# Two model blocks on one core: the high halves of a unit's weights multiplied first, retention keys in blocks of 128, 128 and 16, the last job's halves in one go, and three ring tiles for early expert chunks

## The chip, the core and the metric

The kernel runs on one core of a Trainium2 chip. The core has a matrix engine (PE, with PEld for its weight loads), a vector engine (DVE), a scalar engine (ACT), a general engine (POOL) and a queue engine (SP) that issues most of the transfers; 16 DMA engines move the data. The metric is the device time of one launch in microseconds (us). The profile is one further execution of the same program.

## The reference, cut to what matters

Everything is in float32. The first block takes 256 tokens behind 16 meta tokens (T = 272 rows of 1024) and the second block takes the 256 tokens that come out.

```
def first_block(...):                          # one layer
    u = rmsnorm(h, mix_norm_w);  proj = u @ w_in
    q, k, v, g_ret, lru_in, lru_gate, gate_a, gate_b = split(proj)
    q, k = rotary(q), rotary(k) * 128 ** -0.5          # 8 heads of 128
    o = chunk_retention(q, k, v)                        # causal, decay per head
    y_ret = (silu(g_ret) * head_norm(o)) @ w_branch_ret
    y_lru = (gelu(lru_gate) * rg_lru(conv(lru_in))) @ w_branch_lru
    h = h + (sigmoid(gate_a) * y_ret + sigmoid(gate_b) * y_lru) @ w_out
    g, up = split(rmsnorm(h, ffn_norm_w) @ w_ffn_in)
    h = h + (silu(g) * up) @ w_ffn_out
    return rmsnorm(h, final_norm_w)[:, 16:]

def second_block(x, ...):                      # one layer
    h = x + hybrid_mixer(rms_norm(x), ...)     # mLSTM and a gated spatial mix, then w_out
    # 32 experts (1024 -> 512 -> 1024) in 4 groups, 2 experts per token
    h = h + hierarchical_moe(rms_norm(h), ..., w_gate, w_up, w_down)
    return rms_norm(h, final_g)
```

Without its chunks, one head of retention is: row t of the output is the sum over s <= t of decay^(t-s) (q_t . k_s) v_s, for 272 keys and the 256 queries that are kept.

## The kernel before, in words

**The dense part** holds all of the first block and the second block's mixer, to about 632 us. Its weights are stored as chunks of 1 MB that SP loads in order into a ring of five tiles, `raw` (`load_to`, L147). A chunk is two units of 128 x 1024. ACT rounds a unit to `whi` (L161, four buffers), and DVE, or POOL for units 2 and 5, subtracts that from the chunk to get `wlo` (L167, three buffers). A unit is 24 matmuls on PE: for each of eight slices k of the contraction, the high half of the weights times the high half of the input, the high half times the input's low half, and the low half times the input's high half (`mm3`, L233). `proj` calls `mm3` for some 124 of the units; the others use code of their own. What a unit's result needs afterwards runs behind a later unit.

In the first units the input itself is split slice by slice, by ACT (`FR`, L278) and DVE (L279), while PE uses it. POOL also multiplies the rotary tables COS and SIN by a norm (L290, L291) before it splits unit 5.

**Retention** runs with two heads interleaved, in four pairs, between units. `f0` multiplies K and Q, `f1` scales and masks the products on ACT and DVE into `sw`, and `f2` multiplies by the values. The 272 keys stand as 16 + 128 + 128, the 16 keys of the meta tokens first, so each head has five matmuls in `f2`: 16, 128, 16, 128 and 128 keys deep.

**The expert part** streams the chosen experts' weights, 1 MB chunks again, in one fixed order on SP (`ex`, L1078). A chunk takes the next of 18 fresh buffers, which are tiles that the dense part has finished with (four `raw2`, `FR2`, `FR3`, then `xg`, `yy` and `lb` of a pool that opens late, five ring `raw` tiles, `FR1`, and three pairs of `whi` and `wlo` tiles); after the 18th it takes a buffer that a finished job has given back. `before_wo(i)` calls `ex` between the last dense units. A job is one chunk column (g, c) for a group of tokens: c from 0 to 3 are the gate and up products (L1683), 4 and 5 the down products (L1710 to L1717) followed by scaling (L1736, L1737) and a matmul that adds the rows back into the residual (L1746 to L1748). The first job is (0, 0).

**The end.** The last job is done in two halves of 256 columns. Then the final norm takes sums of squares (L1650 on DVE, L1652 on ACT), POOL multiplies the residual by the gain (L1656), the sums are added (L1779, L1780), root and reciprocal follow, the rows are scaled (L1921 to L1926) and four transfers go out on SP (L1928).

Of the kernel before, what the change touches and what calls it, by code (L numbers as in the profile page):

```python
# [11 lines left out]
F32 = mybir.dt.float32  # L12
# [9 lines left out]
D = 1024  # L22
# [17 lines left out]
HOLD = 5  # L40
WARM = 16
# [58 lines left out]
def _build(tc, nc, h, out, ctx, dbg, stop):  # L100
# [156 lines left out]
    RST = PA.tile([128, TT], F32, name="RST")  # L257
    SP.dma_start(COS, h["rope"][0])
# [35 lines left out]
    def proj(xh, xl, c0, n, *stages, adv=1, tag=None, before=None, ps=ps_mm):  # L294

        o = {}

        def mm(hi, lo):
            p = o["p"] = ps()
            for k in range(8):  # L300
                mm3(p[:, :n], hi[:, k * 128:k * 128 + 128], lo[:, k * 128:k * 128 + 128],
                    xh[:, k, c0:c0 + n], xl[:, k, c0:c0 + n], k == 0, k == 7)
        unit(mm, [lambda f=f: f(o["p"]) for f in stages], adv, tag=tag, before=before)
# [116 lines left out]
    def v_evac(m):  # L420
# [6 lines left out]
        def g(p):  # L427
            t = o["t"]
            q = o["q"] = ps_tp()
            PE.transpose(q[:, 0:128], t[:, NM:NM + 128], ident)  # L430
            PE.transpose(q[:, 128:256], t[:, NM + 128:], ident)
            PE.transpose(q[0:NM, 256:384], t[:, 0:NM], ident)
# [81 lines left out]
    def ret(hd):  # L514
        o = {}
        e = slice(hd * 128, hd * 128 + 128)

        def f0():
            p = o["p"] = ps_sa()
            p2 = o["p2"] = ps_tp()  # L520
            PE.matmul(p[:, 0:256], K[:, hd, NM:NM + 128], Q[:, hd], start=True, stop=True)
            PE.matmul(p[:, 256:384], K[:, hd, NM + 128:], Q[:, hd, 128:], start=True, stop=True)
            PE.matmul(p2[0:NM, 0:256], K[:, hd, 0:NM], Q[:, hd], start=True, stop=True)

        def f1():
            p, p2 = o["p"], o["p2"]
            w = o["w"] = PA.tile([128, 384], F32, name="sw", bufs=2)
            wm = o["wm"] = PA.tile([NM, 256], F32, name="swm", bufs=2)
            S.activation(w[:, 128:256], p[:, 128:256], AF.Copy, scale=vt("gk", 8 + hd))
            S.activation(wm, p2[0:NM, 0:256], AF.Copy, scale=vt("gk", hd)[0:NM])  # L530
            V.scalar_tensor_tensor(w[:, 0:128], p[:, 0:128], vt("gk", 8 + hd), tri, OP.mult, OP.mult)
            V.scalar_tensor_tensor(w[:, 256:384], p[:, 256:384], vt("gk", 16 + hd), tri, OP.mult, OP.mult)

        def f2():
            w, wm = o["w"], o["wm"]
            p = o["p"] = ps_sa()
            PE.matmul(p[:, 0:128], wm[:, 0:128], VM[:, e], start=True, stop=False)
            PE.matmul(p[:, 0:128], w[:, 0:128], VV[:, 0, e], start=False, stop=True)
            PE.matmul(p[:, 128:256], wm[:, 128:256], VM[:, e], start=True, stop=False)
            PE.matmul(p[:, 128:256], w[:, 128:256], VV[:, 0, e], start=False, stop=False)  # L540
            PE.matmul(p[:, 128:256], w[:, 256:384], VV[:, 1, e], start=False, stop=True)
# [470 lines left out]
    for g in range(NG):  # L1012
# [22 lines left out]
                  + [lambda n=n: [fl2(P0.tile([128, 8, TT], F32, name=n))] for n in ("FR2", "FR3")]  # L1035
                  + [lambda: [fl(B["PD"].tile([128, 8, 256], F32, name="xg", bufs=2))],
                     lambda: [fl(B["PD"].tile([128, 4, 512], F32, name="yy"))],
                     lambda: [B["PD"].tile([128, 2048], F32, name="lb")]]
                  + [lambda: [ring.tile([128, 2048], F32, name="raw")]] * RING
# [4 lines left out]
    once = (RING2 + 2, RING2 + 3)  # L1044
# [293 lines left out]
    def before_wo(i):  # L1338
        def f():
            ex(RING2 + 2)  # L1340
            if i == 4:
                need("x1")
                lg["p"] = ps_tp()
        return f
# [299 lines left out]
    def squares(i, c0, n):  # L1644

        for t in range(2):
            x = HB[:, t, c0:c0 + n]
            jk = fl(PD.tile([128, 2, T], F32, name="sg", bufs=2))[:, 0:n]
            if t:
# [101 lines left out]
    def group_job(g, c):  # L1751
# [164 lines left out]
    for t in range(2):  # L1916
        S.activation(rq[:, t:t + 1], rf[:, t, 2:3], AF.Sqrt, scale=1.0 / D, bias=rf[:, t, 0:1])
    for t in range(2):
        r = rq[:, t:t + 1]
        V.reciprocal(r, r)  # L1920
        S.activation(HB[:, t, 0:512], HB[:, t, 0:512], AF.Copy, scale=r)  # L1921
        V.scalar_tensor_tensor(HB[:, t, 768:1024], HB[:, t, 768:1024], r, fing[:, 768:1024], OP.mult, OP.mult)  # L1922
        if t:
            S.activation(HB[:, t, 512:768], HB[:, t, 512:768], AF.Copy, scale=r)
        else:
            V.tensor_scalar(HB[:, t, 512:768], HB[:, t, 512:768], r, None, OP.mult)  # L1926
        for c in (slice(0, 512), slice(512, 1024)):
            SP.dma_start(out[0, t * 128:t * 128 + 128, c], HB[:, t, c])  # L1928
# [35 lines left out]
def pack(inp):  # L1964
    f = np.float32
    a = {k: np.asarray(v) for k, v in inp.items()}
    for k in a:
        if k not in ("x", "meta_tokens", "final_norm_w", "final_g_2"):
# [37 lines left out]
    gk = np.stack([np.exp(-(p - mid)[:, None] * lg), np.exp(-(p + NM - mid)[:, None] * lg),  # L2006
                   np.exp(-(p + NM + 128 - mid)[:, None] * lg)], axis=1) * 128.0 ** -0.5
# [71 lines left out]
```

## Time and profile before

| what | before |
|---|---|
| three runs, median | 1061.01 us (1057.22, 1061.01, 1061.42) |
| profiled execution, its own time | 1060.79 us |
| its span in the trace | 1059.1 us |
| PE busy in the span | 968.0 us (91%) |
| DVE, ACT, POOL busy | 530.3, 408.4 and 64.2 us |
| moved by DMA | 294.96 MB, mean 279 GB/s |

The span is the stretch that the trace covers; the execution's own time is 1.7 us longer. Busy time is the sum over the whole span, which holds two stretches of different kind: the dense part to about 632 us and the expert part after it.

### The profile page before, as it was taken

Reading aid. Unit: us, or ns where it says so; the run is one execution under the profiler, and the core shown is the slowest. Engines: PE = TensorE matmul, PEld = TensorE weight load, DVE = VectorE, ACT = ScalarE, POOL = GpSimd, SP = SyncE. Lnnn points to the kernel's source line nnn. Section 1 sums busy time; section 2 is a strip of 40 time slices with the busy share of each in tenths; the row PEclk is TensorE's granted clock in tenths of the full one; section 3 lists DMA queues with packets and bytes.
Section 4 is the critical chain, followed back from the end, with each engine's and each line's share of the span. In section 5 each row is a group of like instructions: output and inputs, shape, how many; then the busy total and the mean of one; then the engine's idle time right before and its main releaser. Section 6 shows DMA issues by size and latency. Waiting matters only on the chain. (4 is left out here: it accounts for less than half of the span.)

```text
span 1059.1 us, 19506 instructions
## 1 busy us (share of the span) xinstructions
PE 968.0 (91%) x7888; PEld 766.0 (72%) x7888; DVE 530.3 (50%) x961; ACT 408.4 (39%) x682; POOL 64.2 (6%) x63
## 2 busy tenths in 40 slices
PE   8999999999999999999999999989689768878674
PEld 7999998899999999999988985535344324424222
DVE  6788684467777666666796834322112202112013
ACT  6466863466455444444576632111001000100003
POOL 2137400010000000000200000000000000000001
PEclk9999999999999999999999999999898998989978
DMA  8454453336556555545465599999999999999995
GB/s 340 163 192 164 166 193 120 120 110 234 180 195 218 200 178 181 199 167 192 160 227 211 201 375 419 416 416 416 415 418 416 418 418 416 419 416 418 418 417 200
DMA packets 48378, 294.96 MB, mean 279 GB/s; under 512 B 5397, under 2 KB 7061, under 8 KB 17562
## 3 DMA queue, kind: packets, MB, share of 16 engines
q1 hardware_dynamic: 47992, 293.25, 71.1%
q8 instruction: 64, 1.05, 0.4%
q10 hardware_dynamic: 290, 0.39, 0.1%
q14 instruction: 32, 0.26, 0.1%
HBM read 305.16 MB, written 1.05 MB: 289 GB/s over the span
## 5 line engine op out<-in xcount | busy, mean ns | idle before, releaser
L233 PE MATMUL mm<-FR,whi 128*128 128x256 f32 (+1 forms) x2080 | 380.8, 285 | 3.3 <-ACT FR L278 1.8
L233 PEld LDWEIGHTS mm<-FR,whi 128*128 128x128 f32 x2080 | 323.6, 190 | 6.5 <-ACT FR L278 2.0
L167 DVE TENSOR_TENSOR wlo<-raw,whi 128x1024 fp32r<-128x1024 f32 x188 | 237.8, 1268 | 141.0 <-PE mm L233 73.5
L233 PE MATMUL mm<-FR,wlo 128*128 128x256 f32 (+1 forms) x1040 | 295.4, 284 | 1.5 <-POOL wlo L167 0.8
L161 ACT ACTIVATE whi<-raw 128x1024 fp32r<-128x1024 f32 x190 | 200.2, 1059 | 199.8 <-PE mm L233 144.3
L233 PEld LDWEIGHTS mm<-FR,wlo 128*128 128x128 f32 x1040 | 197.9, 190 | 2.0 <-POOL wlo L167 1.0
L1683 PE MATMUL sa<-raw,xg 128*32 128x256 f32 (+1 forms) x1168 | 150.0, 422 | 23.1 <-DMA raw<-in_we_dram 23.1
L1683 PEld LDWEIGHTS sa<-raw,xg 128*32 128x32 f32 (+1 forms) x1168 | 72.5, 126 | 66.4 <-DMA raw<-in_we_dram 31.2
L1683 PE MATMUL sa<-FR,xg 128*32 128x256 f32 (+1 forms) x448 | 74.6, 424 | 16.2 <-DMA FR<-in_we_dram 16.2
L1694 ACT ACTIVATE ht<-tp 128x128 f32<-128x128 f32 x40 | 11.1, 278 | 178.4 <-PE tp L1693 178.4
L1748 DVE TENSOR_TENSOR XS<-mm,XS 128x512 f32<-128x512 f32 (+1 forms) x42 | 26.0, 660 | 86.4 <-PE mm L1747 86.4
L1737 DVE SCALAR_TENSOR_TENSOR yy<-mm,ws,yy 128x512 fp32r<-128x512 f32 (+1 forms) x20 | 14.7, 735 | 104.3 <-ACT yy L1736 104.3
L1683 PE MATMUL sa<-whi,xg 128*32 128x256 f32 (+1 forms) x272 | 62.2, 410 | 2.2 <-DMA whi<-in_we_dram 2.2
L1683 PEld LDWEIGHTS sa<-FR,xg 128*32 128x32 f32 (+1 forms) x448 | 34.6, 125 | 36.0 <-DMA FR<-in_we_dram 21.8
L1689 DVE TENSOR_TENSOR sg<-sg,sa 128x128 f32<-128x128 f32 x40 | 11.3, 283 | 78.2 <-ACT sg L1688 78.2
L233 PE MATMUL mm<-FL,whi 128*128 128x256 f32 x176 | 49.9, 284 | 0.0
L233 PE MATMUL mm<-FH,wlo 128*128 128x256 f32 x176 | 49.8, 283 | 0.0
L233 PE MATMUL mm<-FH,whi 128*128 128x256 f32 x176 | 49.8, 283 | 0.0
L341 PE MATMUL mm<-FR,whi 128*128 128x256 f32 x256 | 46.5, 283 | 0.0
L1688 ACT ACTIVATE sg<-sa 128x128 f32<-128x128 f32 x40 | 11.0, 276 | 85.7 <-PE sa L1683 85.4
L233 PE MATMUL mm<-whi,FR 128*128 128x512 f32 x128 | 41.5, 406 | 0.0
L341 PEld LDWEIGHTS mm<-FR,whi 128*128 128x128 f32 x256 | 39.2, 188 | 0.6 <-issue 0.5
(460 smaller groups left out, 1449.4 us busy)
## 6 DMA issues: line engine op xcount, KB each, us to landing
raw<-in_we_dram SPq DMA_DIRECT2D x106, 1024.0 KB, 15.0
raw<-in_wd_dram SPq DMA_DIRECT2D x94, 1024.0 KB, 4.9
FR<-in_we_dram SPq DMA_DIRECT2D x35, 1024.0 KB, 17.4
whi<-in_we_dram SPq DMA_DIRECT2D x46, 512.0 KB, 16.2
lb<-in_we_dram SPq DMA_DIRECT2D x12, 1024.0 KB, 14.9
wlo<-in_we_dram SPq DMA_DIRECT2D x22, 512.0 KB, 14.9
raw<-in_we_dram SPq DMA_DIRECT2D x4, 512.0 KB
raw<-in_wd_dram SPq DMA_DIRECT2D x2, 512.0 KB
```

The source lines that it names most:

```text
L161: S.activation(his[u], half(u), AF.Copy)
L167: (G if u in POOL_LO or u - 2 * nch in POOL_LO else V).tensor_tensor(los[u], half(u), his[u].bitcast(F32), op=OP.subtract)
L233: PE.matmul(o, a, b, start=start and i == 0, stop=stop and i == 2)
L341: PE.matmul(p[:, j * T:j * T + T], w[:, b:b + 128], z[:, k, 0:T], start=k == 0 and j == 0 and x == 0, stop=k == 7 and x == 2, skip_group_c ...
L1683: PE.matmul(p[r, 0:256], x[:, k, r], raw(k * 256, k * 256 + 256), start=k == 0, stop=k == 7)
L1688: S.activation(sg[:, 0:128], p[:, 0:128], AF.Silu)
L1689: V.tensor_tensor(sg[:, 128:256], sg[:, 0:128], p[:, 128:256], op=OP.mult)
L1694: S.activation(ht()[:, c], q[:, 0:128], AF.Copy)
L1737: V.scalar_tensor_tensor(yl, p[:, 0:n], ws[:, 0:1], yh.bitcast(F32), OP.mult, OP.subtract)
L1748: V.tensor_tensor(HB[:, t, c0:c0 + n], o[:, 0:n], HB[:, t, c0:c0 + n], op=OP.add)
```

## The change: what it does

Six edits are made together.

- **A.** `load_to(3)` is called before the loads of COS, SIN and CS.
- **B.** In `proj`, a unit's 16 matmuls with the high half of its weights stand first, and its 8 with the low half after them; nothing else about the products changes.
- **C.** Retention's keys are taken as 128 + 128 + 16. `f0` has moving sizes of 256, 144 and 16 columns in place of 256, 128 and 256. `f1` scales and masks five blocks in place of four and clears two small ones on POOL. `f2` keeps five matmuls of 128 columns a head: 128 keys, 128 keys for the last 32 rows, 128, 128, and 16 keys for the last 32 rows. The table of decays `gk` and the values' transposes are ordered to suit.
- **D.** `EARLY = 3`: three of the five ring `raw` tiles stand ahead of `xg`, `yy` and `lb` among the fresh buffers, and `before_wo(2)` to `before_wo(4)` may each issue one of them.
- **E.** In the last job the second half's matmuls stand ahead of the first half's adding back; the load of the root's table stands earlier; POOL takes the gain for the first 512 columns alone; the two small additions of sums are gone.
- **F.** The final norm has one sum over the three partial sums, one root and one reciprocal for both row blocks; ACT scales 512 columns and DVE scales the other 512 with the gain; one of the four output transfers is issued by ACT.

```diff
+EARLY = 3
...
+    load_to(3)
     SP.dma_start(COS, h["rope"][0])
...
         def mm(hi, lo):
             p = o["p"] = ps()
+            b = lambda w, k: w[:, k * 128:k * 128 + 128]
             for k in range(8):
-                mm3(p[:, :n], hi[:, k * 128:k * 128 + 128], lo[:, k * 128:k * 128 + 128],
-                    xh[:, k, c0:c0 + n], xl[:, k, c0:c0 + n], k == 0, k == 7)
+                for i, x in enumerate((xh, xl)):
+                    PE.matmul(p[:, :n], b(hi, k), x[:, k, c0:c0 + n], start=k == 0 and i == 0, stop=False)
+            for k in range(8):
+                PE.matmul(p[:, :n], b(lo, k), xh[:, k, c0:c0 + n], start=False, stop=k == 7)
...
         def f0():
             p = o["p"] = ps_sa()
-            p2 = o["p2"] = ps_tp()
-            PE.matmul(p[:, 0:256], K[:, hd, NM:NM + 128], Q[:, hd], start=True, stop=True)
-            PE.matmul(p[:, 256:384], K[:, hd, NM + 128:], Q[:, hd, 128:], start=True, stop=True)
-            PE.matmul(p2[0:NM, 0:256], K[:, hd, 0:NM], Q[:, hd], start=True, stop=True)
+            PE.matmul(p[:, 0:256], K[:, hd, 0:128], Q[:, hd], start=True, stop=True)
+            PE.matmul(p[:, 256:400], K[:, hd, 128:256], Q[:, hd, 112:], start=True, stop=True)
+            PE.matmul(p[0:NM, 400:416], K[:, hd, T:], Q[:, hd, T - NM:], start=True, stop=True)
...
+            G.memset(w[:, 256:272], 0.0)
+            G.memset(w[0:NM, 416:432], 0.0)
+            S.activation(w[:, 112:256], p[:, 112:256], AF.Copy, scale=gA)
+            S.activation(w[:, 400:416], p[:, 384:400], AF.Copy, scale=gB)
+            V.scalar_tensor_tensor(w[:, 0:112], p[:, 0:112], gA, tri[:, 16:128], OP.mult, OP.mult)
+            V.scalar_tensor_tensor(w[:, 272:400], p[:, 256:384], gB, tri, OP.mult, OP.mult)
+            V.scalar_tensor_tensor(w[0:NM, 432:448], p[0:NM, 400:416], gC, tri[0:NM, 0:NM], OP.mult, OP.mult)
...
         def f2():
...
-            PE.matmul(p[:, 0:128], wm[:, 0:128], VM[:, e], start=True, stop=False)
-            PE.matmul(p[:, 0:128], w[:, 0:128], VV[:, 0, e], start=False, stop=True)
-            PE.matmul(p[:, 128:256], wm[:, 128:256], VM[:, e], start=True, stop=False)
-            PE.matmul(p[:, 128:256], w[:, 128:256], VV[:, 0, e], start=False, stop=False)
-            PE.matmul(p[:, 128:256], w[:, 256:384], VV[:, 1, e], start=False, stop=True)
+            last = slice(96, 128)
+            PE.matmul(p[:, 0:128], w[:, 0:128], VV[:, 0, e], start=True, stop=False, skip_group_check=True)
+            PE.matmul(p[last, 0:128], w[:, 256:288], VV[:, 1, e], start=False, stop=True, skip_group_check=True)
+            PE.matmul(p[:, 128:256], w[:, 128:256], VV[:, 0, e], start=True, stop=False, skip_group_check=True)
+            PE.matmul(p[:, 128:256], w[:, 288:416], VV[:, 1, e], start=False, stop=False, skip_group_check=True)
+            PE.matmul(p[last, 128:256], w[0:NM, 416:448], VM[:, e], start=False, stop=True, skip_group_check=True)
...
+                  + [lambda: [ring.tile([128, 2048], F32, name="raw")]] * EARLY
                   + [lambda: [fl(B["PD"].tile([128, 8, 256], F32, name="xg", bufs=2))],
...
-                  + [lambda: [ring.tile([128, 2048], F32, name="raw")]] * RING
+                  + [lambda: [ring.tile([128, 2048], F32, name="raw")]] * (RING - EARLY)
...
-            ex(RING2 + 2)
+            ex(RING2 + 2 + max(0, min(i - 1, EARLY)))
...
         mm, e0, e1 = down_steps(hts[g], *prep[g], 512, 256)
+        V.memset(rq, 1.0)
+        S.activation(rq, rq, AF.Sqrt)
         mm(parts)
         flush()
         e0()
-        V.memset(rq, 1.0)
-        S.activation(rq, rq, AF.Sqrt)
         mm_, e0_, e1_ = down_steps(hts[g], *prep[g], 768, 256, exact=True)
-        e1()
         mm_(parts)
         squares(0, 0, 512)
         gain(0, 512)
-        squares(1, 512, 256)
-        gain(512, 256)
-        x = rf[:, :, 0]
-        V.tensor_tensor(x, x, rf[:, :, 1], op=OP.add)
-        V.tensor_scalar(x, x, 1.0 / D, EPS, OP.mult, OP.add)
-        return e0_, e1_
+        e0_()
+        e1()
+        squares(1, 512, 256, True)
+        return (e1_,)
...
-    for t in range(2):
-        S.activation(rq[:, t:t + 1], rf[:, t, 2:3], AF.Sqrt, scale=1.0 / D, bias=rf[:, t, 0:1])
+    V.tensor_reduce(rq, rf, AX.X, OP.add)
+    S.activation(rq, rq, AF.Sqrt, scale=1.0 / D, bias=vt("eps"))
+    V.reciprocal(rq, rq)
     for t in range(2):
         r = rq[:, t:t + 1]
...
+        a, b = slice(0, 512), slice(512, 1024)
+        S.activation(HB[:, t, a], HB[:, t, a], AF.Copy, scale=r)
+        V.scalar_tensor_tensor(HB[:, t, b], HB[:, t, b], r, fing[:, b], OP.mult, OP.mult)
+        for i, c in enumerate((a, b)):
+            (S if t and not i else SP).dma_start(out[0, t * 128:t * 128 + 128, c], HB[:, t, c])
```

Where two heads' `f2` stand on PE, these are one head's five matmuls before (the last column is the weights' partitions by the moving columns).

```order
L537 MATMUL sa<-VM,swm 128x128
L538 MATMUL sa<-VV,sw 128x128
L539 MATMUL sa<-VM,swm 128x128
L540 MATMUL sa<-VV,sw 128x128
L541 MATMUL sa<-VV,sw 128x128
```

The same place on PE after the change.

```order
L546 MATMUL sa<-VV,sw 128x128
L547 MATMUL sa<-VV,sw 32x128
L548 MATMUL sa<-VV,sw 128x128
L549 MATMUL sa<-VV,sw 128x128
L550 MATMUL sa<-VM,sw 32x128
```

The number of matmuls and their moving columns stay, two of them now write 32 rows, and the one 16 keys deep stands last alone instead of at two places.

On SP, where the last dense chunks give way to the first expert chunks, the loads stood like this (`in_wd` are dense chunks, `in_we` expert chunks).

```order
L147 DMA raw<-in_wd_dram 128x2048 x2
L1078 DMA raw_6603<-in_we_dram 128x2048
L1078 DMA FR_6605<-in_we_dram 128x2048
L1078 DMA FR_6607<-in_we_dram 128x2048
L1078 DMA xg<-in_we_dram 128x2048
L1078 DMA yy<-in_we_dram 128x2048
L1078 DMA lb<-in_we_dram 128x2048
L1078 DMA raw<-in_we_dram 128x2048 x5
L1078 DMA FR_6892<-in_we_dram 128x2048
```

After the change they stand like this.

```order
L1088 DMA raw_6611<-in_we_dram 128x2048
L1088 DMA FR_6613<-in_we_dram 128x2048
L1088 DMA FR_6615<-in_we_dram 128x2048
L1088 DMA raw<-in_we_dram 128x2048 x3
L1088 DMA xg<-in_we_dram 128x2048
L1088 DMA yy<-in_we_dram 128x2048
L1088 DMA lb<-in_we_dram 128x2048
L1088 DMA raw<-in_we_dram 128x2048 x2
L1088 DMA FR_6900<-in_we_dram 128x2048
```

Three loads into ring tiles now stand ahead of those into `xg`, `yy` and `lb`; the number of loads before the first reuse of a buffer is the same.

## Rows read from the trace of the kernel before

**Rows 1.** The page: 40 slices of the span, busy tenths.

```profile
PE   8999999999999999999999999989689768878674
DMA  8454453336556555545465599999999999999995
```

**Rows 2.** Windows: engine busy us (x), granted PE clock, DMA share, GB/s.

```profile
595.00:600.50 5.50, 5.50 (x50) 5.50 (x49) 5.27 (x8) 4.69 (x7) 0.58 (x1) 1.00 0.02 6
...
633.00:634.00 1.00, 1.00 (x24) 0.63 (x20) 0.92 (x5) 0.70 (x2) 0.00 (x0) 1.00 0.53 78
...
634.00:1041.00 407.00, 335.39 (x2928) 161.98 (x2919) 84.72 (x236) 43.92 (x128) 0.00 (x0) 0.93 1.01 416
```

**Rows 3.** Timeline of SP's queue, 586 to 634 us: start, us, issue.

```profile
618.57 2.67 SPq L1078 DMA_DIRECT2D wlo<-in_we_dram  x2
632.63 0.80 SPq L1078 DMA_DIRECT2D raw<-in_we_dram  x2
```

**Rows 4.** Timeline of PE, 628 to 634 us.

```profile
628.96 3.66 PE L1683 MATMUL sa<-raw,xg 128*32 128x256 f32 x64
```

**Rows 5.** PE's waits, 0 to 632 us: us in total, times, longest.

```profile
PE tp L233 <- POOL wlo L167: 1.1, 1, 1.1
...
PE mm L233 <- DVE wlo L167: 1.0, 2, 0.7
```

**Rows 6.** Timeline of DVE (first row) and PE, 7 to 18 us.

```profile
8.43 3.40 DVE L279 SCALAR_TENSOR_TENSOR FR<-XS,VT,FR 128x272 fp32r<-128x272 f32 x8
...
12.29 0.52 PE L233 MATMUL mm<-FR,whi 128*128 128x272 f32 x2
13.55 0.40 PE L233 MATMUL mm<-FR,wlo 128*128 128x272 f32 x1 [0.74 <-DVE wlo L167]
...
16.05 0.42 PE L233 MATMUL mm<-FR,whi 128*128 128x272 f32 x2
...
16.43 0.41 PE L233 MATMUL mm<-FR,whi 128*128 128x272 f32 x2
17.64 0.39 PE L233 MATMUL mm<-FR,wlo 128*128 128x272 f32 x1 [0.79 <-POOL wlo L167]
```

**Rows 7.** Timeline of PE: a pair's `f0` at 186, part of its `f2` at 195.

```profile
186.41 0.59 PE L521 MATMUL sa<-Q,K 128*128 128x256 f32 x2
186.84 0.38 PE L522 MATMUL sa<-Q,K 128*128 128x128 f32 x2
187.16 0.60 PE L523 MATMUL tp<-Q,K 128*16 128x256 f32 x2
187.69 0.70 PE L521 MATMUL sa<-Q,K 128*128 128x256 f32 x2
...
195.78 0.48 PE L539 MATMUL sa<-VM,swm 16*128 16x128 f32 x2
196.20 0.49 PE L540 MATMUL sa<-VV,sw 128*128 128x128 f32 x2
196.52 0.39 PE L541 MATMUL sa<-VV,sw 128*128 128x128 f32 x2
196.84 0.48 PE L537 MATMUL sa<-VM,swm 16*128 16x128 f32 x2
```

**Rows 8.** Window around the second pair's `f2`.

```profile
178.00:184.00 6.00, 6.00 (x36) 5.76 (x36) 1.08 (x3) 1.16 (x7) 0.00 (x0) 0.72 0.43 164
```

**Rows 9.** Timeline of the end, 1047 to 1055 us.

```profile
1047.70 3.57 POOL L1656 TENSOR_TENSOR XS<-XS,H 128x1024 f32<-128x1024 f32 x2 [446.17 <-DVE sg L1650]
...
1048.10 1.97 DVE L1779 TENSOR_TENSOR rf<-rf 128x2 f32<-128x2 f32 x1 [0.29 <-ACT sg L1652]
...
1048.87 1.13 PE L1744 MATMUL mm<-sg,pm 128*128 128x256 f32 x4 [0.56 <-ACT sg L1733]
...
1051.21 0.74 DVE L1748 TENSOR_TENSOR XS<-mm,XS 128x256 f32<-128x256 f32 x2
...
1054.26 0.49 ACT L1924 ACTIVATE XS<-XS,rq 128x256 f32<-128x256 f32 x1
```

More of the change, by code (lines that the diff above doesn't have):

```diff
@@ L429, in g @@
             q = o["q"] = ps_tp()
-            PE.transpose(q[:, 0:128], t[:, NM:NM + 128], ident)
-            PE.transpose(q[:, 128:256], t[:, NM + 128:], ident)
-            PE.transpose(q[0:NM, 256:384], t[:, 0:NM], ident)
+            PE.transpose(q[:, 0:128], t[:, 0:128], ident)
+            PE.transpose(q[:, 128:256], t[:, 128:256], ident)
+            PE.transpose(q[0:NM, 256:384], t[:, T:], ident)
         def e(p):
@@ L525, in f1 @@
+            PE.matmul(p[0:NM, 400:416], K[:, hd, T:], Q[:, hd, T - NM:], start=True, stop=True)
         def f1():
[L526 to L531, printed above, removed]
@@ L532, in f1 @@
-            V.scalar_tensor_tensor(w[:, 256:384], p[:, 256:384], vt("gk", 16 + hd), tri, OP.mult, OP.mult)
+            p = o["p"]
+            w = o["w"] = PA.tile([128, 448], F32, name="sw", bufs=2)
+            gA, gB, gC = vt("gk", 8 + hd), vt("gk", 16 + hd), vt("gk", hd)[0:NM]
+            G.memset(w[:, 256:272], 0.0)
+            G.memset(w[0:NM, 416:432], 0.0)
+            S.activation(w[:, 112:256], p[:, 112:256], AF.Copy, scale=gA)
+            S.activation(w[:, 400:416], p[:, 384:400], AF.Copy, scale=gB)
@@ L534, in f2 @@
+            V.scalar_tensor_tensor(w[:, 0:112], p[:, 0:112], gA, tri[:, 16:128], OP.mult, OP.mult)
+            V.scalar_tensor_tensor(w[:, 272:400], p[:, 256:384], gB, tri, OP.mult, OP.mult)
+            V.scalar_tensor_tensor(w[0:NM, 432:448], p[0:NM, 400:416], gC, tri[0:NM, 0:NM], OP.mult, OP.mult)
         def f2():
-            w, wm = o["w"], o["wm"]
+            w = o["w"]
             p = o["p"] = ps_sa()
-            PE.matmul(p[:, 0:128], wm[:, 0:128], VM[:, e], start=True, stop=False)
@@ L1042, in _build @@
                      for n in ((("whi", NHI),) * 2, (("whi", NHI),) * 2, (("wlo", NLO),) * 2)])
-    once = (RING2 + 2, RING2 + 3)
+    once = (RING2 + 2 + EARLY, RING2 + 3 + EARLY)
     def ex(n=len(loads)):
@@ L1642, in fing_rows, with squares @@
         S.activation(fing[:, c], p, AF.Copy)
-    def squares(i, c0, n):
+    def squares(i, c0, n, act=False):
         for t in range(2):
@@ L1648, in squares @@
             jk = fl(PD.tile([128, 2, T], F32, name="sg", bufs=2))[:, 0:n]
-            if t:
+            if t and not act:
                 V.scalar_tensor_tensor(jk, x, 1.0, x, OP.mult, OP.mult, accum_out=rf[:, t, i:i + 1])
@@ L1915, in _build @@
     squares(2, 768, 256)
-    for t in range(2):
-        S.activation(rq[:, t:t + 1], rf[:, t, 2:3], AF.Sqrt, scale=1.0 / D, bias=rf[:, t, 0:1])
+    V.tensor_reduce(rq, rf, AX.X, OP.add)
+    S.activation(rq, rq, AF.Sqrt, scale=1.0 / D, bias=vt("eps"))
+    V.reciprocal(rq, rq)
     for t in range(2):
         r = rq[:, t:t + 1]
[L1920 to L1928, printed above, removed]
+        a, b = slice(0, 512), slice(512, 1024)
[3 more added lines that the diff above has]
+            (S if t and not i else SP).dma_start(out[0, t * 128:t * 128 + 128, c], HB[:, t, c])
 def _units(w):
@@ L2005, in pack @@
     mid = TT / 2
-    gk = np.stack([np.exp(-(p - mid)[:, None] * lg), np.exp(-(p + NM - mid)[:, None] * lg),
-                   np.exp(-(p + NM + 128 - mid)[:, None] * lg)], axis=1) * 128.0 ** -0.5
+    gk = np.stack([np.exp(-(p + T - mid)[:, None] * lg), np.exp(-(p - mid)[:, None] * lg),
+                   np.exp(-(p + 128 - mid)[:, None] * lg)], axis=1) * 128.0 ** -0.5
     gt = np.stack([np.exp((p + NM - mid)[:, None] * lg), np.exp((p + NM + 128 - mid)[:, None] * lg)], axis=1)
```

## The prediction

> **What bounds the kernel now.** I read the page's slices first, because the kernel has two stretches with different limits. PE is 90% busy or more in nearly all of the first 24 slices, and DMA in nearly all of the last 17 [rows 1]. Then I read the windows. From 634 to 1041 us DMA runs at a share of 1.01 and 416 GB/s, while PE is busy for 335 of 407 us [rows 2]. So PE sets the pace before 632 us, DMA from 634 to 1041, and a chain of small steps after that.
>
> The next question decides most of the sum: what sets the moment at which the DMA stretch begins? SP's queue answers it. The pair of `wlo` tiles is the 18th and last fresh buffer, and it is issued at 618.57; the next load, into a tile that has been used, is issued at 632.63 [rows 3]. Between 628.96 and 632.62 PE runs the first job, (0, 0) [rows 4]. So the first reuse waits for PE to finish that job, and in the meantime DMA runs dry: 78 GB/s in the microsecond from 633 [rows 2]. I call the end of that job T0. At T0 all 18 buffers are full and what is still to come is the same list of chunks at 416 GB/s. Whatever PE saves before T0 therefore moves T0, the DMA stretch and the end by as much; a transfer that is only moved to before T0 makes DMA run dry sooner, and moves nothing.
>
> **B, the order in a unit.** Three of the first units make PE wait for a low half that comes late. Unit 1 starts at 12.29 with high halves, and its first low-half matmul stands at 13.55; unit 2 starts at 16.43 and stands still until 17.64 [rows 6]. A group of three matmuls takes 16.43 - 16.05 = 0.38 us, or 0.127 each [rows 6], so without waiting the low half would stand 0.25 us after each start: 1.0 us is lost in each of the two. Unit 5 loses 1.1 us, to POOL's subtraction [rows 5]. Two waits on DVE's `wlo` add to 1.0, 0.7 at most [rows 5]; the second, 0.3, lies in a later unit. That is 3.4 us.
>
> With the 16 high matmuls first, the low half is wanted 2.0 us (16 x 0.127) after a unit's start, against 0.25. Unit 1's is there after 1.26 (13.55 - 12.29), unit 2's after 1.21. Unit 5's comes from POOL, which waits for the first norm; that norm's matmul stands behind unit 2 and so moves forward with PE, and POOL with it. All three waits should go.
>
> Against this stands unit 0. There the input's halves come slice by slice, the last from DVE at 8.43 + 3.40 = 11.83 [rows 6]. Today a slice's three matmuls follow each slice. After the change the eight low-half matmuls are left over for the end: 11.83 + 2 x 0.127 + 8 x 0.127 = 13.1, where unit 1 starts at 12.29 now. That costs 0.8. Net: 3.4 - 0.8 = 2.6 us, bounds 1.3 (unit 5's wait stays, and the small one) and 3.4. Everywhere else the same 24 matmuls run. In a group of three the weights stay once and change twice, and its 0.38 us is little more than 3 x 272 columns take at a column a cycle and 2.4 GHz (0.34), so little is left that fewer changes could save or more could cost; I take nothing for the order itself.
>
> **A.** The two early chunks are issued ahead of the rotary tables. PE's first units wait for splits and not for chunks [rows 5, 6]; the tables are used only after the first norm. Nothing either way; if the cover were gone, POOL would be late by the 2 MB, 5.0 us at 416 GB/s [rows 2], and unit 5's wait of 1.1 would stay.
>
> **C, retention.** PE is never idle here, so columns count. In `f0` a head takes 187.69 - 186.41 = 1.28 us: 0.43 for 256 columns, 0.32 for 128, and 0.53 for the 16 keys by 256 columns [rows 7]. The last becomes 16 x 16, the second grows to 144 columns. By columns alone (0.43 for 256) 144 take 0.24, and the step next to a narrow form has about 0.1 on top (0.32 against 0.21), so 0.34. For the 16 x 16 the trace has no row. It lies between 0.1, the surcharge alone, and 0.32, the row of 128 columns; I take 0.2, nearer to the surcharge since columns hardly count. A head saves 0.02 less than 0.33, that is 0.3, and eight heads 2.5 (bounds 1.5 and 3.3).
>
> In `f2` five matmuls of 128 columns remain. A narrow one (16 keys) takes 0.42, a wide one followed by a wide one 0.32 [rows 7]. Before, two of five are narrow and they stay two; the new ones write 32 rows, so they load a quarter of the weights. If a narrow one still costs 0.42 nothing is gained; if it costs only its columns (0.21), 2 x 0.21 x 8 = 3.4 is. I take 1.4, a little under half, because switches of form stay as many. C is 3.9 us, bounds 1.5 and 6.7. The two clears on POOL and the extra operation on DVE lie beside PE: both have whole units between `f0` and `f2`.
>
> The Trainium skill speaks against this part: TensorEngine Tiling (Array Packing), section Key Properties, says that changing the tiling mode drains TensorE. The trace agrees with it as far as it goes, by the 0.1 us that a step next to a narrow one has on top. By that rule alone, with as many switches as before, `f2` would give nothing and the sum would be 1.4 smaller.
>
> The clock can move this term. Around the second pair's `f2` the granted clock is 0.72 over 6 us, that is 1.7 us lost, in part at the 1.2 GHz level [rows 8]; a like stretch follows the fourth pair, none the first and third. All of them come behind `f2`. I leave both as they are; each that goes or comes moves the time by 1.7.
>
> **D, early ring tiles.** From 595 to 600.5 us DMA is nearly idle (6 GB/s) [rows 2], since `xg` waits for its pool. Three chunks of 1 MB, 2.5 us each at 416 GB/s, can use that gap. By the gate above this gives nothing: the 18 buffers are full sooner, and the 19th load still waits for T0. I take 0, bounds 0 and, if the early bytes did count, 7.5.
>
> **E and F, the tail.** DVE adds two numbers for 1.97 us (1048.10) while POOL's gain runs from 1047.70 to 1051.27, and its next adding back starts at 1051.21, though PE had the sums at 1048.87 + 1.13 = 1050.0 [rows 9]. With the two small additions gone and POOL on half of its work (1.8 us, to 1049.5), the adding back takes 0.74 from 1049.7, as it can begin when the first block's product is there, and ends at 1050.45. Then follow a square (0.5), the sum, root and reciprocal (0.2, 0.3 and 0.2), and two scalings of 512 columns on ACT (1.5, beside DVE's two): 1053.15. Today the last scaling ends at 1054.26 + 0.49 = 1054.75 [rows 9]. The gain is 1.6 us, bounds 0.5 and 3.3 (the second half's matmuls can also start earlier, if their data is there).
>
> The Trainium skill, SBUF — State Buffer, section Who interferes with whom, says that a DVE instruction with two inputs in SBUF contends with a GpSimd one that reads there. The trace agrees: 1.97 us for 128 x 2 numbers. By that rule the removal of those additions is the part of E that pays.
>
> **Sum.** 2.6 + 0 + 3.9 + 0 + 1.6 = 8.1. The profiled execution took 1060.79 us, 0.2 under the median of 1061.01; 1060.79 - 8.1 = 1052.7, say 1052.5 us.
>
> **The rivals.**
>
> - The early bytes count: the gate is not PE's first job but DMA's own backlog. The DMA that runs dry at 633 speaks against it. It would give 1052.5 - 7.5 = 1045. Chance 0.07. The Trainium skill's DMA: Bandwidth & Descriptors, section Rules for kernel authors, advises issuing a DMA early so that its fixed cost lies beside work; here it would do what this rival says.
> - What PE gains does not arrive at T0, because some later wait in the dense part, on an engine that keeps its own pace, takes it back; only the tail's 1.6 and part of C remain, 1057 to 1059. For it: PE's waits are few only because the others are just ahead. Against it: DMA is half idle and PE full for hundreds of microseconds [rows 1]. Chance 0.14.
> - Slower: the order of B costs cadence. Some 124 units of 24 matmuls are 2976 matmuls; each nanosecond more on one costs 3.0 us. From 2.7 ns on, the 8.1 us are eaten, and from 4.5 ns the kernel is 0.5% slower; 6 ns would add 17.9 and give 1070. For it: every matmul loads weights under the one before, and runs of the same kind now follow each other. Against it: the step of 0.127 leaves little room [rows 6]. Chance 0.04.
> - The clock drops after all four `f2` pairs, or after none: plus or minus 3.4, that is 1056 or 1049. This is inside the range.
>
> **How the numbers follow.** The forecast holds with 0.75. Its own range is 1048 to 1056, from the bounds of B, C and the tail and one clock stretch. For 8 in 10, I widen it by a little on either side, 1046 to 1057.5: the first rival and the slower one are left out, as is half of the second. About 0.5%, 5.3 us, is what a measurement of this kernel can tell from no change. Faster by more (below 1055.7): most of the forecast and the first rival, 0.76. Same: the second rival and the forecast's upper end, 0.20. Slower: 0.04.
>
> **What would show it.** Right: the waits on `wlo` in units 1, 2 and 5 are gone and unit 1 starts near 13.1; a head's `f0` takes about 1.0; PE's first expert job ends some 6.5 us earlier, with a stall of DMA before it that is longer than now; from there to the last landing the same 407 us or so; the adding back starts near 1049.7 less the shift. Wrong: T0 stays, or the time from T0 to the last landing changes, or matmuls of the units of 272 columns stand more than 0.127 apart.

## The result and the profile after

Four runs of the changed kernel took 1048.36 to 1049.11 us, median 1048.99; the kernel before took 1057.22 to 1061.42 beside them, median 1061.02. The ratio is 0.9900, with a 95% interval of 0.9882 to 0.9917. In later groups of runs the kernel before had medians of 1057.35 to 1059.00, so against those the gain would have been 8.4 to 10.0 us. The profiled execution took 1049.08 us with a span of 1047.4 us, 11.7 less than before.

PE is now full for nearly all of the first 23 slices of the page, and DMA for nearly all of the last 17.

```profile
PE   9999999999999999999999999989688778878775
...
DMA  8545453446556555545463979999999999999995
```

**The gate.** SP's queue answers to [rows 3], PE's timeline to [rows 4], the windows to [rows 2].

```profile
607.12 0.97 SPq L1088 DMA_DIRECT2D wlo<-in_we_dram  x2
620.95 5.05 SPq L1088 DMA_DIRECT2D raw<-in_we_dram  x4
```

```profile
617.27 3.66 PE L1693 MATMUL sa<-raw,xg 128*32 128x256 f32 x64
```

```profile
618.00:621.00 3.00, 3.00 (x60) 1.64 (x52) 0.00 (x0) 1.29 (x2) 0.00 (x0) 1.00 0.00 0
623.00:1029.00 406.00, 337.51 (x2914) 164.43 (x2902) 84.38 (x236) 44.13 (x130) 0.00 (x0) 0.91 1.01 417
```

The first reuse of a buffer is again issued when PE ends its first job, now at 620.95 instead of 632.63. The gain at T0 is 11.68 us and the gain of the span is 11.7. In the three microseconds from 618 DMA moves nothing at all, where before it ran dry for a shorter time. From T0 to the end it takes 426.4 us in the kernel before and 426.5 in the changed one.

**The first units.** These are the rows that answer to [rows 6].

```profile
8.05 3.82 PE L305 MATMUL mm<-FR,whi 128*128 128x272 f32 x16 [0.89 <-ACT FR L280]
11.71 1.16 PE L307 MATMUL mm<-FR,wlo 128*128 128x272 f32 x8
12.71 2.18 PE L305 MATMUL mm<-FR,whi 128*128 128x272 f32 x16
14.73 1.16 PE L307 MATMUL mm<-FR,wlo 128*128 128x272 f32 x8
15.72 2.18 PE L305 MATMUL mm<-FR,whi 128*128 128x272 f32 x16
17.74 1.16 PE L307 MATMUL mm<-FR,wlo 128*128 128x272 f32 x8
```

Units 1, 2 and 5 no longer wait for a low half; the small wait of 0.3 us in a later unit, which is between 400 and 560 us, is still there. Unit 0 takes 4.66 us, against 3.84 before; units 1 and 2 take 3.0 each, which is 24 matmuls at 0.126. But later in the dense part PE stands twice inside one unit, the first of the mix behind retention; in the kernel before it stood there once, for 0.31 us, on DVE.

```profile
236.57 0.39 PE L305 MATMUL mm<-FR,whi 128*128 128x256 f32 x1 [0.41 <-ACT FR L590]
237.29 0.62 PE L305 MATMUL mm<-FR,whi 128*128 128x256 f32 x3 [0.34 <-DVE FR L593]
```

**Retention.** A pair's `f0` and the second head of a pair's `f2`, as in [rows 7].

```profile
179.32 0.60 PE L526 MATMUL sa<-Q,K 128*128 128x256 f32 x2
179.75 0.41 PE L527 MATMUL sa<-Q,K 128*128 128x144 f32 x2
180.09 0.21 PE L528 MATMUL sa<-Q,K 128*16 128x16 f32 x2
180.23 0.70 PE L526 MATMUL sa<-Q,K 128*128 128x256 f32 x2
...
188.62 0.49 PE L546 MATMUL sa<-VV,sw 128*128 128x128 f32 x2
189.04 0.41 PE L547 MATMUL sa<-VV,sw 128*32 128x128 f32 x2
189.37 0.49 PE L548 MATMUL sa<-VV,sw 128*128 128x128 f32 x2
189.70 0.39 PE L549 MATMUL sa<-VV,sw 128*128 128x128 f32 x2
190.02 0.40 PE L550 MATMUL sa<-VM,sw 16*32 16x128 f32 x2
190.35 1.21 PE L305 MATMUL mm<-FR,whi 128*128 128x256 f32 x8
```

A head's `f0` takes 180.23 - 179.32 = 0.91 us, against 1.28. The narrow matmuls of `f2` take 0.33 each (189.37 - 189.04, 190.35 - 190.02). And the granted clock no longer falls: over the whole of retention it is 1.00 now. The two rows below are the same stretch of the program, from the first `f0` to behind the last `f2`, of the kernel before and of the changed one.

```profile
149.05:220.20 71.15, 71.15 (x484) 62.44 (x483) 34.26 (x57) 27.11 (x63) 0.00 (x0) 0.95 0.34 124
```

```profile
145.69:209.40 63.71, 63.71 (x485) 56.75 (x483) 35.13 (x65) 24.56 (x64) 0.89 (x12) 1.00 0.40 138
```

**The end.** The rows that answer to [rows 9]. The first is where PE takes up the last chunk, which is the last load to land.

```profile
1035.35 0.40 PE L1727 MATMUL mm<-whi,ht 128*32 128x256 f32 x1 [0.64 <-DMA whi<-in_we_dram]
...
1035.41 2.36 POOL L1666 TENSOR_TENSOR XS<-XS,H 128x1024 f32<-128x1024 f32 x1 [445.56 <-DMA whi<-in_we_dram]
...
1037.73 1.75 DVE L1758 TENSOR_TENSOR XS<-mm,XS 128x256 f32<-128x256 f32 x4 [2.56 <-PE mm L1757]
...
1040.86 1.41 DVE L1930 SCALAR_TENSOR_TENSOR XS<-XS,rq,H 128x512 f32<-128x512 f32 x2
...
1040.91 1.33 ACT L1929 ACTIVATE XS<-XS,rq 128x512 f32<-128x512 f32 x2 [0.29 <-DVE rq L1925]
...
1041.66 1.34 SPq L1932 DMA_DIRECT2D out_dram<-XS  x3
```

In the kernel before, PE takes up the last chunk here.

```profile
1046.39 0.40 PE L1717 MATMUL mm<-whi,ht 128*32 128x256 f32 x1
```

The two small additions beside POOL are gone. The row at 1037.73 holds the adding back of both halves; the second half's starts at 1038.63, by the chain that ended last.

```profile
1038.63 0.42 DVE XS L1758
```

The last scaling ends at 1042.27. Counted from the last chunk's matmul, that is 6.92 us (1042.27 - 1035.35), against 8.36 before (1054.75 - 1046.39). Less than half of these 1.44 us reaches the end of the span, which comes 12.07 us after that matmul, against 12.66: 0.6. And the matmul itself comes 0.64 us later after T0 than before (414.40 against 413.76), so that in this pair the two cancel.

### The profile page after: what moved, and what is told of

The parts are those of the page before. It is cut to its first block, busy times and chain, and to the rows that moved or that the text cites. A ratio compares the mean times of both kernels' runs of the same rounds, so it can differ in the third digit from the quotient of the medians.

```text
span 1047.4 us, 19533 instructions
## 1 busy us (share of the span) xinstructions
PE 962.3 (92%) x7888; PEld 760.5 (73%) x7888; DVE 529.0 (51%) x964; ACT 406.0 (39%) x682; POOL 65.0 (6%) x78
## 5 line engine op out<-in xcount | busy, mean ns | idle before, releaser
L305 PE MATMUL mm<-FR,whi 128*128 128x256 f32 (+1 forms) x1920 | 253.4, 284 | 1.8 <-ACT FR L280 0.9
L305 PEld LDWEIGHTS mm<-FR,whi 128*128 128x128 f32 x1920 | 238.3, 188 | 4.6 <-ACT FR L280 1.1
L1693 PE MATMUL sa<-raw,xg 128*32 128x256 f32 (+1 forms) x1200 | 152.9, 426 | 25.6 <-DMA raw<-in_we_dram 18.3
L307 PE MATMUL mm<-FR,wlo 128*128 128x256 f32 (+1 forms) x960 | 134.0, 282 | 0.0
L307 PEld LDWEIGHTS mm<-FR,wlo 128*128 128x128 f32 x960 | 122.9, 189 | 0.0
L1720 PE MATMUL mm<-raw,ht 128*32 128x512 f32 (+1 forms) x176 | 37.5, 662 | 3.8 <-DMA raw<-in_we_dram 3.8
L1693 PEld LDWEIGHTS sa<-whi,xg 128*32 128x32 f32 (+1 forms) x272 | 28.7, 123 | 16.9 <-DMA whi<-in_we_dram 4.5
## 6 DMA issues: line engine op xcount, KB each, us to landing
lb<-in_we_dram SPq DMA_DIRECT2D x12, 1024.0 KB, 13.1
```

The costliest lines, as they stand in the source:

```text
L305: PE.matmul(p[:, :n], b(hi, k), x[:, k, c0:c0 + n], start=k == 0 and i == 0, stop=False)
L307: PE.matmul(p[:, :n], b(lo, k), xh[:, k, c0:c0 + n], start=False, stop=k == 7)
L1693: PE.matmul(p[r, 0:256], x[:, k, r], raw(k * 256, k * 256 + 256), start=k == 0, stop=k == 7)
L1720: PE.matmul(y, x, raw(m * 512, m * 512 + 512), start=m == 0, stop=m == 3)
```

## The experiments

T0 below is the issue of the first load into a buffer that has been used. "Lower clock" are the stretches of 3.4 us before T0 in which the granted clock was at its 1.2 GHz level in the profiled execution, by their start.

| kernel | median (fastest), us | T0 | span's end after T0 | lower clock before T0 |
|---|---|---|---|---|
| before | 1061.02 (1057.22) | 632.63 | 426.4 | 179, 216, 561, 619 |
| changed | 1048.99 (1048.36) | 620.95 | 426.5 | none |
| e1, without B | 1052.25 (1050.91) | 627.21 | 426.7 | 553, 618 |
| e2, without C | 1055.50 (1054.34) | 627.03 | 425.8 | 617 |
| e3, without D | 1050.33 (1049.00) | 622.60 | 426.1 | 613 |
| e4, without E and F | 1050.81 (1049.25) | 621.14 | 427.6 | none |
| e5, mixed order | 1048.09 (1047.38) | 620.00 | 425.7 | none |
| e6, before again | 1058.65 (1055.93) | 632.49 | 426.4 | 161, 198, 560 |
| e7, 48 matmuls more, dense | 1062.50 (one run) | 635.04 | 425.8 | 11, 626 |
| e8, 48 matmuls more, expert | 1049.07 (one run) | 621.39 | 426.0 | 607 |
| e9, only B | 1056.01 (1053.64) | 628.52 | 426.6 | 212, 556 |
| e10, only C | 1051.71 (1051.43) | 623.66 | 426.2 | 609 |
| e11, without C again | 1054.39 (one run) | 626.88 | 425.8 | 193, 613 |

The kernel before ran beside them with 1055.5 to 1064.8 us; its medians were 1058.97 beside e1 to e4, 1059.00 beside e5 to e8 and 1057.35 beside e9 to e11.

**e1, without B.**

```diff
-            for k in range(8):
-                for i, x in enumerate((xh, xl)):
-                    PE.matmul(p[:, :n], b(hi, k), x[:, k, c0:c0 + n], start=k == 0 and i == 0, stop=False)
-            for k in range(8):
-                PE.matmul(p[:, :n], b(lo, k), xh[:, k, c0:c0 + n], start=False, stop=k == 7)
+            for k in range(8):
+                mm3(p[:, :n], hi[:, k * 128:k * 128 + 128], lo[:, k * 128:k * 128 + 128],
+                    xh[:, k, c0:c0 + n], xl[:, k, c0:c0 + n], k == 0, k == 7)
```

> Everything of the change but B: proj goes back to three matmuls a slice. Theory 1 (the dense part is a plain sum, and B is worth the waits in units 1, 2 and 5): unit 5 ends 2.6 to 3.1 us later than in the changed kernel, the granted clock before the first expert job stays at full speed, and the time is 1049.0 + 3 = 1052. Theory 2 (the order of B is also what keeps the granted clock up in the dense part): four stretches at the lower clock come back, 1.7 us each, and the time is 1049.0 + 3 + up to 6.8, some 1057 to 1059.

The waits of PE in the dense part are those of the kernel before again [rows 5].

```profile
PE tp L234 <- POOL wlo L168: 1.1, 1, 1.1
...
PE mm L234 <- DVE wlo L168: 1.0, 2, 0.7
PE mm L234 <- POOL wlo L168: 0.8, 1, 0.8
```

Counted from the start of unit 0, the first matmul behind unit 5 (PE's 177th) starts after 22.70 us here and after 19.94 in the changed kernel: B is worth 2.76 there. Up to the end of retention this grows to 3.0 in small steps. The stretch that holds the first unit of the mix is 0.7 us shorter here than in the changed kernel, so B gives that back. At PE's 4,199th matmul, some 519 us into the program, its net is 2.35 us (521.91 - 8.80 against 518.81 - 8.05). The median is 3.3 over the changed kernel's, and two stretches at the lower clock are in the profile, at 553 and 618, so theory 1 was right on B and not on the clock; theory 2 was not borne out, as none came back in retention.

**e2 and e11, without C.** The edit puts the retention of before into the changed kernel.

```diff
-            PE.matmul(p[:, 256:400], K[:, hd, 128:256], Q[:, hd, 112:], start=True, stop=True)
-            PE.matmul(p[0:NM, 400:416], K[:, hd, T:], Q[:, hd, T - NM:], start=True, stop=True)
+            PE.matmul(p[:, 256:384], K[:, hd, NM + 128:], Q[:, hd, 128:], start=True, stop=True)
+            PE.matmul(p2[0:NM, 0:256], K[:, hd, 0:NM], Q[:, hd], start=True, stop=True)
...
```

> Everything of the change but C: retention's keys as 16 + 128 + 128 again. Theory 1 (plain sum): four pairs of heads at 1.1 us each come back and no lower clock, 1049.0 + 4.4 = 1053.4. Theory 2 (the old retention is what the granted clock falls after): two stretches at the lower clock behind the second and the fourth pair as well, 1.7 us each, 1049.0 + 4.4 + 3.4 = 1056.8.

> The changed kernel without C once more, for a second profile. Theory 3: a stretch at the lower clock behind some pair of the old f2, and T0 1.5 us later for each. Theory 4: again none between 140 and 230 us.

In e2 the same stretch of retention runs at full clock throughout, so it gives the price of C's matmuls alone.

```profile
145.91:214.00 68.09, 68.09 (x485) 59.38 (x484) 34.26 (x57) 26.89 (x64) 0.00 (x0) 1.00 0.37 130
```

That is 68.1 against 63.7 us: C's matmuls give 4.4. The stretch of the kernel before took 71.15, so 3.1 of its time was the clock. In e2's profile the clock did not fall in retention, and theory 1 seemed right; but the ten timed runs spread over 3.2 us, which a plain sum doesn't explain, and the second profile (e11) has such a stretch behind the third pair's `f2`.

```profile
192.00:198.00 6.00, 6.00 (x34) 5.64 (x34) 0.85 (x2) 1.83 (x9) 0.00 (x0) 0.72 0.51 178
```

**e3, without D.**

```diff
-EARLY = 3
+EARLY = 0
```

> The changed kernel with EARLY = 0, so xg, yy and lb stand ahead of the ring tiles again. Theory 1 (the end of PE's first expert job sets the DMA stretch): DMA moves little from 583 to 588 us and runs dry for a shorter time before that job's end, and the time stays at 1049.0 within 0.7. Rival (early bytes count): up to 7.5 us later, 1056.5.

DMA is nearly idle from 583 to 589 us here, as it was before in its like stretch; in the changed kernel it moved 388 GB/s then. It has less of a dry stretch ahead of T0.

```profile
583.00:589.00 6.00, 6.00 (x54) 6.00 (x53) 5.77 (x9) 5.14 (x7) 0.63 (x1) 1.00 0.07 29
...
614.00:619.00 5.00, 5.00 (x36) 4.61 (x39) 0.97 (x6) 1.87 (x6) 0.00 (x0) 0.76 1.02 407
```

T0 is 1.65 later: 0.13 is a later start, and 1.5 comes with a stretch at the lower clock at 613, which e2 and e11, with D, have as well (617 and 613). From T0 to the end it takes 426.1 us. So the 3 MB that are moved ahead change nothing after T0. The fastest run is 1049.0. The rival's 1056.5 is out.

**e4, without E and F.**

```diff
-        e0_()
-        e1()
-        squares(1, 512, 256, True)
-        return (e1_,)
+        squares(1, 512, 256)
+        gain(512, 256)
...
+        V.tensor_tensor(x, x, rf[:, :, 1], op=OP.add)
+        V.tensor_scalar(x, x, 1.0 / D, EPS, OP.mult, OP.add)
+        return e0_, e1_
...
```

> The changed kernel with the old last job and old final norm. Theory 1, from the two traces: from the landing of the first half's last chunk to the end of the span it took 17.8 us before and 17.1 after, so the time is 1049.0 + 0.7 = 1049.7. Rival, as predicted: 1.6 us, 1050.6. If the tail is worth nothing: 1049.0.

T0 is that of the changed kernel within 0.2, no clock fell before it, and from T0 to the end it takes 427.6 us instead of 426.5. The first output transfer is issued 421.8 us after T0 here and 420.7 in the changed kernel. Over all the profiles of this study that time is 420.8 to 421.8 in the five with the old end (mean 421.1) and 420.0 to 420.9 in the eight with the new one (mean 420.3), so E and F give 0.8 up to that issue. Most of the scatter in these numbers is when the last chunk lands. PE takes it up 413.6 to 414.6 us after T0, whichever end the kernel has; from there the first output transfer is issued after 7.16 to 7.20 us in the five and after 6.31 or 6.32 in the eight, so that the gain is 0.87, and the last scaling ends after 8.33 to 8.36 and after 6.92. The median is 1.8 higher, but the runs spread over 3 us; the profiles' 0.87 is the better number, near theory 1.

**e5, mixed order.** The first unit of all and the first of the mix keep three matmuls a slice; all others have B's order.

```diff
-    def proj(xh, xl, c0, n, *stages, adv=1, tag=None, before=None, ps=ps_mm):
+    def proj(xh, xl, c0, n, *stages, adv=1, tag=None, before=None, ps=ps_mm, each=False):
...
+            if each:
+                for k in range(8):
+                    mm3(p[:, :n], hi[:, k * 128:k * 128 + 128], lo[:, k * 128:k * 128 + 128],
+                        xh[:, k, c0:c0 + n], xl[:, k, c0:c0 + n], k == 0, k == 7)
+                return
...
-             ps=ps_tp if 4 <= m < 6 else ps_mm)
+             ps=ps_tp if 4 <= m < 6 else ps_mm, each=m == 0)
...
-        proj(CH, CL, 0, T, ev, tag="mix")
+        proj(CH, CL, 0, T, ev, tag="mix", each=m == 0)
```

> The changed kernel, but with three matmuls a slice in the two units whose input halves come slice by slice while PE is already there: the first unit and the first unit of the mix after retention. Theory 1 (B gives 2.75 us in units 1, 2 and 5 and 0.7 is lost again in the mix unit, where the changed kernel waits 0.41 and 0.34): unit 1 starts 0.8 us sooner after unit 0's start, the two waits in the mix unit go, and the time is 1049.0 - 1.5 = 1047.5. Rival (what PE gains is taken back by the next wait): 1049.0.

T0 comes at 620.00, 0.95 earlier than in the changed kernel, and the six runs have a median of 1048.09. The wait in the mix unit shrinks from two to one.

```profile
237.02 0.39 PE L234 MATMUL mm<-FR,whi 128*128 128x256 f32 x1 [0.31 <-DVE FR L598]
```

Unit 1 starts at 11.86 instead of 12.71, but by unit 6 only 0.3 of that is left: theory 1 is right in the mix unit, and the rival for more than half of the first one. This is the fastest version by 0.9 us; the two kernels were not timed side by side, so that the difference is no more than the profiles' T0 and the medians say.

**e6, the kernel before again.**

> The kernel before, unchanged, for a second profile. Theory 1 (the stretches at the lower clock in the dense part come by the run, up to some four of 1.7 us in this kernel): another number of such stretches or other places than 179, 216, 561 and 619 us, and times spread over 1055.5 to 1062. Rival (they belong to the old retention and to fixed places): the same four places.

The stretches lie behind the first and the third pair of heads now, at 161 and 198, and not behind the second and the fourth.

```profile
160.00:165.00 5.00, 5.00 (x28) 4.76 (x28) 0.85 (x2) 0.74 (x6) 0.00 (x0) 0.66 0.52 200
197.50:203.00 5.50, 5.50 (x34) 5.34 (x33) 0.85 (x2) 0.69 (x6) 0.00 (x0) 0.69 0.44 179
```

So which pairs are hit changes from run to run; that it is behind an `f2` does not. Both theories had half of it.

**e7 and e8, 48 more matmuls.** The same lines stand once ahead of one of the last dense units and once ahead of a job in the expert part; what they write is not used.

```diff
+            q = ps_tp()
+            for _ in range(48):
+                PE.matmul(q[:, 0:128], ones, ones, start=True, stop=True)
```

> The changed kernel with 48 more matmuls of 128 columns on PE before one of the last dense units; their result is not used. They take 10 to 16 us of PE. Theory 1 (the end of PE's first job sets the DMA stretch): the first reload of a buffer and the end come later by what they take. Rival (DMA's own backlog): the end moves by at most half of it, since all the early chunks can land meanwhile.

> The changed kernel with the same 48 more matmuls in the expert part, ahead of the first column of the sixth group. Theory 1 (DMA sets the pace there, PE has 15 to 25% to spare): the time stays at 1049 within 1.5. Rival (PE's work counts there as well): 10 to 16 us later.

Here are their matmuls in the two traces; one stands as two instructions.

```profile
L1354 PE MATMUL tp<-ones x96: 270/275/275, 588.6 to 599.2; 128*128 128x128 f32 x96
```

```profile
L1768 PE MATMUL tp<-ones x96: 275/275/275, 785.5 to 796.1; 128*128 128x128 f32 x96
```

They take 10.6 us of PE in the one and 10.8 in the other. In the dense part T0 moves to 635.04, by 14.1, and the end of the span by 13.4. Of the 14.1, 10.6 are theirs and the rest is two stretches at the lower clock (11 and 626 us) and a start that is 0.7 later. In the expert part the time is 1049.07: nothing of them is seen. Theory 1 on the gate is shown from both sides.

**e9 and e10, B and C alone.** Each puts one part of the change into the kernel before, with no other edit.

> The kernel before with B alone. The plain sum: the kernel before without a stretch at the lower clock in its dense part takes some 1056, B gives 2.0, so the fastest runs take 1054. Theory 3 (the old f2 is what the clock falls behind, whatever the order of the units): one or two stretches behind pairs of f2 in the profile, runs spread over 4 us and more, median 1056 to 1057. Theory 4 (the old order of the units has a part in it): none behind f2, median under 1055.

> The kernel before with C alone. The plain sum: 1056 - 4.0 = 1052 for the fastest runs. Theory 3: no stretch at the lower clock between 140 and 230 us, median within 1.7 of the fastest (one near 560 or 617 us may remain). Theory 4: such stretches remain in retention, median 1054 or more.

With B alone the fastest run is 1053.64, against 1055.52 for the kernel before beside it: 1.9 us. The median moves by only 1.3, the runs spread over 4.8 us, and the clock falls behind the last pair's `f2`.

```profile
211.00:216.00 5.00, 5.00 (x30) 4.88 (x30) 0.61 (x2) 1.27 (x5) 0.00 (x0) 0.66 0.49 195
```

With C alone the fastest run is 1051.43, 4.1 us below; the median is 5.6 below, the six runs lie within 1.6 us, and retention runs at full clock though the units have their old order.

```profile
148.76:212.50 63.74, 63.74 (x484) 56.80 (x483) 35.13 (x65) 24.87 (x63) 0.89 (x12) 1.00 0.39 137
```

Theory 3 holds in both, and theory 4 in neither.

## Why the prediction was right

The forecast was 1052.5 us in a range of 1046 to 1057.5, and 1048.99 came. The direction, the gate and two of the three sums were right; one term that was set to nothing was the largest miss. The prediction's own sum was 8.1 us; that 12.0 came is in part chance, since the medians of the kernel before in later groups are 2.0 to 3.7 us lower than the one beside it.

**The gate held.** T0 moved by 11.68 us and the span by 11.7. In all kernels but e4, whatever their T0 between 620 and 635 us, the end came 425.7 to 426.7 us after it. e7 and e8 show it with the same work on either side, and e3 shows that early bytes are worth nothing. The rivals "the early bytes count" and "what PE gains does not arrive" are out.

**The account up to T0.** Up to the first job both programs have the same number of matmuls on PE, 4,806, so a matmul of the one can be set beside the matmul of the same number in the other. The first row below is the 4,199th and the second begins with the 4,739th; the kernel before stands first, then the changed one.

```profile
528.90 0.63 PE L233 MATMUL mm<-whi,FR 128*128 128x512 f32 x2
...
618.81 3.40 PE L1466 MATMUL mm<-CS,H 128*128 128x128 f32 x16
```

```profile
518.81 0.63 PE L234 MATMUL mm<-whi,FR 128*128 128x512 f32 x2
...
607.13 1.94 PE L1476 MATMUL mm<-CS,H 128*128 128x128 f32 x16
...
610.70 0.18 PE L1444 MATMUL tp<-EB,triB 128*128 128x32 bf16 x1 [1.58 <-DVE EB L1491]
```

Counted from the start of unit 0, the 4,199th starts after 520.45 us before and after 510.76 in the changed kernel, 9.69 apart. It starts after 513.11 in e1 and after 515.12 in e2, so 2.35 of this is B and 4.36 is C. The 2.98 that are left are the two stretches at the lower clock in retention, 1.49 each; e11, which has one, is 1.50 behind e2, which has none. At the second row the two kernels are 11.68 apart: 0.40 is the earlier start of unit 0, 9.69 the above, and 1.59 comes with the stretch at 561. That is all of T0's gain. The stretch at 619 costs nothing there: it makes the 16 matmuls take 3.40 us instead of 1.94, but at full clock PE then stands 1.58 for DVE.

**B, forecast 2.6, measured 2.75 at the units that it was argued from, and 2.35 in all.** Unit 1 starts at 12.71 and not at 13.1 because unit 0 began 0.4 us earlier; the profiles show that start between 8.0 and 8.8, so this 0.4 is not the change's, and A shows no effect. The sum came out near for other parts than it was made of: the 0.3 of a later unit did not go, while units 1, 2 and 5 gave 1.1, 1.1 and 1.4 where 1.0, 1.0 and 1.1 were counted. What the step lacked is the second place where PE meets an input that is still being split: the mix's first unit. With the high halves first PE comes to the last slices after 12 matmuls and not after 18, and waits 0.41 and 0.34 where it waited 0.31. The same sentence that priced unit 0 should have been asked of every unit that starts on fresh input.

**C, forecast 3.9, measured 4.4 for its matmuls** (e2 against the changed kernel; e10 against before by the fastest runs 4.1). A head's `f0` gives 0.37, a little over the 0.3 forecast, which is 3.0 for eight: the 16 x 16 takes 0.14 (180.23 - 180.09) where 0.2 was taken. A pair's `f2` goes from 3.60 us (194.95 to 198.55 before) to 3.35 (187.00 to 190.35), and the matmul ahead of it from 0.21 to 0.12, which together is 1.4 for four pairs, as forecast. The narrow matmuls of 32 rows take 0.33 where those of 16 keys took 0.42 [rows 7], so the bound of "still 0.42" was too dark, and `f2` gave its 1.4 with as many changes of form as before. One reading behind the `f0` sum does not hold: the 0.32 of 128 columns was put down to the narrow step next to it, but in `f2` a wide matmul followed by a wide one takes 0.32 as well [rows 7].

**The clock was the term that was mis-sized.** The step said "I leave both as they are", 0 us with 1.7 either way for each. Both went, at 1.5 each. The step also read that all such stretches come behind `f2`, and the same trace has two more before T0, at 561 and 619; the one at 561 went too. In the profiled pair of executions the clock is 4.6 us of the 11.7. The prediction had the case without the two in retention among its rivals, as "after none", at 1049. How many stretches an execution has varies: the two profiles of the kernel before have four and three. The fastest of its 61 timed runs took 1055.52 and the fastest of the changed kernel 1048.36, 7.2 apart, and B, C and the 0.6 of the end are 7.3; so the fastest runs fit executions without a costly stretch, which is argued, as timed runs have no trace.

What the runs show of its cause is this. With the old `f2` the clock fell behind at least one pair in four of five profiles (before, e6, e9 and e11, not e2), in either order of the units. With the new one it fell behind none in eight (changed, e1, e3, e4, e5, e7, e8 and e10). So the retention stretches belong to C, and C's full value by medians is 5.6 us (e10), the 4.4 and some 1.2 on average for the clock. What in the old `f2` or `f0` does it was not tried apart. A stretch near 555 us stands in four profiles (before, e1, e6 and e9), none of them of a kernel with both B and C; that is too few to call it the change's. Those near 615 us (607 to 626) come in eight of thirteen, with and without each part of the change, and cost up to 1.6 at T0 (e1). The cause of both stays open.

**E and F, forecast 1.6, measured 1.44 at the last scaling, 0.87 at the first output transfer and 0.6 at the end.** The stall was read rightly: 1049.7 is 3.31 us behind the last chunk's matmul (1046.39), and the second half's adding back starts 3.28 behind it (1038.63 - 1035.35). The failed step is that this was counted to the last scaling. The output is 1 MB that begins to move after the first issue, and that issue, which stood 1.16 us ahead of the last scaling's end, now stands only 0.61 ahead. From it to the end of the span it then takes 5.75 us instead of 5.46; it took 5.76 in e4 too, with the old end, so that this 0.3 is not E's or F's, and what it belongs to stays open. In the profiled pair the 0.6 does not show, because the last chunk was taken up 0.64 later after T0. That time is 413.6 to 414.6 us in the thirteen profiles and follows no part of the change: e5 and e8, which have all of it but the order of two units or some matmuls more, stand at 413.65 and 413.95.

**A and D: nothing, as forecast.** A was not tried alone; unit 0 starts at 7.97 to 8.45 us in the four profiles without it and at 8.02 to 8.80 in the nine with it. D moved 3 MB ahead and DMA ran dry for them.

## What to carry to other kernels

Where two stretches follow each other with different limits, look for the one event that hands over, and price every edit by whether it moves that event: some 11 us of matmuls moved the end by at least as much ahead of it and by nothing behind it. The same goes for a slow stretch: 1.5 us of it counted in full in retention and not at all where PE would have waited for DVE. An order that suits a late weight does not suit a late input, so ask of every unit that starts on fresh input which operand comes last. And where the granted clock is below full in a stretch that an edit rewrites, give the clock its own term with a chance, instead of leaving it as it was.

## What was not expected of the hardware

- A few matmuls can come with a cost larger than their own: behind some pairs of the old retention the granted clock fell to the 1.2 GHz level for 3.4 us while PE was busy throughout, 1.5 us lost each time, and which pairs changed between two executions of the same program (179 and 216 us, 161 and 198).
- A narrow matmul of retention took 0.33 us where it writes 32 rows (16 or 128 keys deep), and 0.42 where it writes 128 rows from 16 keys.
- The first matmul of the first unit started between 7.97 and 8.80 us in thirteen profiles whose programs are the same up to there or nearly so.
